# Attention's sums with the values taken over four query blocks instead of two, with the transposes one step later

## The chip, the core and the metric

The kernel runs on one core of a Trainium2 chip. The engines named here are PE (the matrix engine, TensorE), ACT (ScalarE), DVE (VectorE), POOL (GpSimd) and SP, which only issues DMAs. Each engine works through a queue of its own, in the order in which its instructions stand there. The metric is the device time of one execution in microseconds (us), taken as the median of several runs; lower is better.

## What is computed

One layer of a Griffin-style block on 1024 positions of width 1024, in float32: a stick-breaking attention with 16 heads of 64 channels and a gated short convolution side by side, each projected and gated, then an output projection and a SwiGLU FFN. The change concerns the attention:

```python
for i in range(s_len // Q_BLOCK):              # 8 query blocks of 128
    n_keys = (i + 1) * Q_BLOCK                 # causal: the keys up to and with this block
    z = einsum('bhqd,bhkd->bhqk', q[block i], k[:n_keys]) / sqrt(64)
    mask = s_idx < t_idx                       # strictly causal
    log_not = where(mask, log_sigmoid(-z), 0.0)
    excl = cumsum(log_not, reverse=True) - log_not
    a = where(mask, exp(log_sigmoid(z) + excl), 0.0)
    o[block i] = einsum('bhqk,bhkd->bhqd', a, v[:n_keys])
y = (sigmoid(ga) * (o @ w_branch_a) + sigmoid(gb) * (y_b @ w_branch_b))
```

## The kernel before

Every large product is made in split arithmetic: an operand is held as a high part (rounded to the engine's fp32r format) and a low part (the rest), and a product is the sum of two or three matmuls of 128 rows by up to 512 columns. A matmul with 512 columns is the largest that one PSUM bank takes.

The program is a sequence of stages: modulation and norm, the input projections, the attention (from 596 to 956 us of the span), the projection of branch a (`ya` times `w_a`), the output projection, the FFN. Its instructions are mixed with *fillers*: the convolution's gate and the product of branch b, matmuls of 512 columns into `pj`, in threes (lines 1026 to 1028).

A generator, `attention()`, goes through 128 steps, one for each head h and query block i, and issues in each:

- `att_scores(h, i)`: the scores `z` of block i against keys 0 to i, in pieces of at most 512 keys, two matmuls each (lines 921, 922). Steps i of 0 to 3 have one piece of 128 to 512 columns; steps 4 to 7 have one of 128 to 512 columns and one of 512. Each piece takes one of two PSUM banks (`NZ = 2`) and ACT turns it into sigmoids in `pt` (line 923), which frees the bank. POOL masks the diagonal.
- `att_scan(h, i)`: a running product on DVE (line 936) and one multiplication on POOL (line 133), after which `pt` holds the weights.
- `att_trans` of the step two steps back: PE transposes of those weights, 128x128 each, up to four into a bank `tr` (line 950, `NTR = 3` banks); ACT writes the high part `ath` (line 953) and DVE the low part `atl` (line 954).
- `att_av(h, g)`, three steps behind, in every second step: the sum with the values for the query blocks 2g and 2g+1 into a bank `o` of 256 columns, two matmuls for each key block (lines 965, 966), the stationary operand being the split values `vt` (high and low part side by side in 64 + 64 columns). The last key block concerns only the second query block, so its two matmuls have 128 columns. Then ACT takes out the upper 64 rows, adding `vlast` as bias (two instructions of 64x128, line 970, tile `otmp`), DVE adds the lower 64 rows (line 972, `oy`), and SP stores 64x256 to `d_ya`.

`att_dv` makes the `vt` of the next head in two parts, in steps 3 to 6 of the current one: ACT writes the high part (line 863), DVE the low part. `vt` has two buffers, so head h+1 gets the one that head h-1 used.

Between two yields of the generator the main loop issues fillers: a yield's number is a share of the fillers, and `fill` catches up to it. The order on PE is then pinned as issued, and that of the attention's own instructions on DVE and POOL too; ACT's and SP's order comes from the scheduler, which ranks by priority and expected readiness. Names in rows carry a running number (`z_9560`), which differs between the two builds.

## Time and profile before

| | |
|---|---|
| median of 3 runs (lowest, highest) | 1792.84 us (1792.69, 1794.17) |
| the profiled execution | 1792.41 us |
| its span in the trace | 1790.4 us |
| granted PE clock, mean | 1.00 |
| PE, DVE, ACT, POOL busy over the span | 1782.5, 1273.5, 830.9, 345.0 us |
| PE busy in 700 to 800 us (attention) | 99.87 us |
| DVE, ACT, POOL busy there | 80.09, 70.87, 39.04 us |

The time is what counts; the span is the part of it that the trace covers, and 2.0 us lie around it. Busy times are sums of instructions' durations. PE's instructions are pipelined: the next one starts before the one ahead has ended, so what a matmul costs is read from the distance of one start to the next, and a late operand can show as a long distance without any idle time beside it.

### The profile page before, as it was taken

Reading aid. Unit: us, or ns where it says so; the run is one execution under the profiler, and the core shown is the slowest. Engines: PE = TensorE matmul, PEld = TensorE weight load, DVE = VectorE, ACT = ScalarE, POOL = GpSimd, SP = SyncE. Lnnn points to the kernel's source line nnn. Section 1 sums busy time; section 2 is a strip of 40 time slices with the busy share of each in tenths; the row PEclk is TensorE's granted clock in tenths of the full one; section 3 lists DMA queues with packets and bytes.
Section 4 is the critical chain, followed back from the end, with each engine's and each line's share of the span. In section 5 each row is a group of like instructions: output and inputs, shape, how many; then the busy total and the mean of one; then the engine's idle time right before and its main releaser. Section 6 shows DMA issues by size and latency. Waiting matters only on the chain.

```text
span 1790.4 us, 24937 instructions
## 1 busy us (share of the span) xinstructions
PE 1782.5 (100%) x8611; PEld 1485.4 (83%) x8611; DVE 1273.5 (71%) x2030; ACT 830.9 (46%) x1555; POOL 345.0 (19%) x437
## 2 busy tenths in 40 slices
PE   9999999999999999999999999999999999999999
PEld 7888877888888888888888888888888888888887
DVE  6876586777874678777786864698867777644876
ACT  5534364333433567776675221764544444422321
POOL 0024334734231334333332100100000000000000
PEclk9999999999999999999999999999999999999999
DMA  9479654222634977796655856424534344389876
GB/s 383 162 248 381 240 185 165 77 94 100 225 130 147 298 197 191 218 324 172 166 136 176 308 194 212 129 95 169 208 130 148 147 183 157 137 316 345 276 236 220
DMA packets 165010, 359.09 MB, mean 201 GB/s; under 512 B 15538, under 2 KB 60938, under 8 KB 163732
## 3 DMA queue, kind: packets, MB, share of 16 engines
q1 hardware_dynamic: 128300, 289.65, 49.1%
q10 hardware_dynamic: 33096, 55.25, 8.7%
q0 software_dynamic: 3488, 12.59, 2.0%
q8 instruction: 69, 1.13, 0.3%
q14 instruction: 57, 0.47, 0.1%
HBM read 247.84 MB, written 109.62 MB: 200 GB/s over the span
## 4 chain that ended last, share of the span: by engine, by line
PE 96%; DMA 1%; DVE 1%; issue 0%; ACT 0%; POOL 0%; SPq 0%; POOLq 0%; DVEq 0%; ACTq 0%
PE e L129 8%; PE e L128 8%; PE e L127 8%; PE pj L127 7%; PE pj L128 7%; PE pj L129 7%; PE pj L294 7%; PE pj L1026 5%; PE pj L1028 5%; PE pj L1027 5%; PE e L1618 4%; PE e L1619 4%; PE e L1620 4%; PE tr L950 3%; PE o L966 2%; PE z L921 2%
## 5 line engine op out<-in xcount | busy, mean ns | idle before, releaser
L1234 ACT ACTIVATE whi<-raw 128x512 fp32r<-128x512 f32 x137 | 84.9, 628 | 160.6 <-PE e L128 99.8
L1235 DVE TENSOR_TENSOR wlo<-raw,whi 128x512 fp32r<-128x512 f32 x137 | 93.1, 687 | 70.6 <-ACT whi L1234 53.1
L133 POOL TENSOR_TENSOR pt<-pt 128x63 f32<-128x63 f32 (+7 forms) x128 | 101.6, 794 | 212.1 <-DVE pt L936 195.7
L128 PE MATMUL e<-big,whi 128*128 128x512 f32 x352 | 136.9, 389 | 0.0
L127 PE MATMUL e<-big,whi 128*128 128x512 f32 x352 | 136.5, 390 | 0.0
L129 PE MATMUL e<-big,wlo 128*128 128x512 f32 x352 | 136.1, 389 | 0.0
L294 PE MATMUL pj<-whi,big 128*128 128x512 f32 x448 | 132.6, 393 | 0.6 <-ACT big L263 0.4
L133 DVE TENSOR_TENSOR c<-pj,c 128x512 f32<-128x512 f32 x140 | 93.7, 684 | 53.9 <-PE pj L129 53.3
L954 DVE TENSOR_TENSOR atl<-tr,ath 128x512 fp32r<-128x512 f32 (+1 forms) x192 | 104.1, 553 | 35.6 <-ACT ath L953 34.2
L127 PE MATMUL pj<-big,whi 128*128 128x512 f32 x320 | 124.9, 390 | 0.0
L129 PE MATMUL pj<-big,wlo 128*128 128x512 f32 x320 | 124.7, 390 | 0.0
L128 PE MATMUL pj<-big,whi 128*128 128x512 f32 x320 | 124.6, 389 | 0.0
L1619 PE MATMUL e<-wlo,f 128*128 128x512 f32 (+1 forms) x319 | 121.9, 382 | 0.0
L1618 PE MATMUL e<-whi,f 128*128 128x512 f32 (+1 forms) x319 | 121.7, 382 | 0.0
L1620 PE MATMUL e<-whi,f 128*128 128x512 f32 (+1 forms) x319 | 121.6, 382 | 0.0
L923 ACT ACTIVATE pt<-z,rq 128x128 f32<-128x128 f32 (+1 forms) x192 | 107.2, 578 | 26.3 <-PE z L922 23.8
L524 ACT ACTIVATE whi<-raw 128x512 fp32r<-128x512 f32 x108 | 67.5, 629 | 109.0 <-PE pj L128 54.3
L133 DVE TENSOR_TENSOR wlo<-raw,whi 128x512 fp32r<-128x512 f32 x108 | 89.4, 831 | 36.2 <-ACT whi L524 36.1
L1026 PE MATMUL pj<-big,whi 128*128 128x512 f32 x256 | 113.3, 442 | 0.0
L953 ACT ACTIVATE ath<-tr 128x512 fp32r<-128x512 f32 (+1 forms) x192 | 93.2, 488 | 31.8 <-PE tr L950 30.8
L127 PE MATMUL e<-rh,whi 128*128 128x512 f32 x264 | 102.7, 389 | 0.0
L128 PE MATMUL e<-rl,whi 128*128 128x512 f32 x264 | 102.7, 389 | 0.0
(304 smaller groups left out, 4756.1 us busy)
## 6 DMA issues: line engine op xcount, KB each, us to landing
f<-d_f SPq DMA_DIRECT2D x77, 512.0 KB, 4.2
d_f<-fs SPq DMA_DIRECT2D x70, 512.0 KB, 2.6
raw<-w_cg SPq DMA_DIRECT2D x40, 512.0 KB, 4.1
raw<-w_u SPq DMA_DIRECT2D x26, 512.0 KB, 4.5
raw<-w_g SPq DMA_DIRECT2D x25, 512.0 KB, 3.4
raw<-w_kv SPq DMA_DIRECT2D x20, 512.0 KB, 5.2
ld<-ada SPq DMA_DIRECT2D x16, 512.0 KB, 8.7
d_t<-ts SPq DMA_DIRECT2D x16, 512.0 KB, 6.7
```

The costliest lines, as they stand in the source:

```text
L127: nc.tensor.matmul(ps, wh[:, k, :], fh[:, k, :], start=(k == 0 and not onto), stop=False, skip_group_check=onto)
L128: nc.tensor.matmul(ps, wh[:, k, :], fl[:, k, :], start=False, stop=False, skip_group_check=onto)
L129: last = nc.tensor.matmul(ps, wl[:, k, :], fh[:, k, :], start=False, stop=(k == 3), skip_group_check=onto)
L133: eng.tensor_tensor(out=out, in0=a, in1=b, op=op)
L294: nc.tensor.matmul(ps, a, b, start=(k == 0 and q == 0), stop=(k == KT - 1 and q == 2))
L923: nc.scalar.activation(pt[:, off + s0:off + s0 + m], z[:, :m], AF.Sigmoid, scale=rq[:, 1, i, h:h + 1])
L953: nc.scalar.activation(th[:, :nb, c0:c0 + P], src, AF.Copy)
L954: nc.vector.tensor_tensor(out=tl[:, :nb, c0:c0 + P], in0=src, in1=th[:, :nb, c0:c0 + P].bitcast(F32), op=ALU.subtract)
L1026: nc.tensor.matmul(ps, wh, rh_, start=(k == 0), stop=False)
L1618: nc.tensor.matmul(o, sh, w[0][:, c], start=(j == 0), stop=False)
L1619: nc.tensor.matmul(o, sh, w[1][:, c], start=False, stop=False)
L1620: nc.tensor.matmul(o, sl, w[0][:, c], start=False, stop=(j == NJ - 1))
```

## The change

The sum with the values now covers four query blocks at once (`o` of 512 columns; g is 0 or 1), in one group of key blocks that all four query blocks see (512 columns) and one that ends at the diagonal (512, 384, 256, 128 columns). The transposed weights get tiles of their own for the two groups: `afh`/`afl` (one buffer) for the first, `ath`/`atl` (two buffers) for the second. The transposes stand three steps behind the scores instead of two, and the sums four or more: `att_av` is now a generator that is advanced by pieces of two key blocks, so that the sum for g = 0 is made in step 7 of its head and step 1 of the next one, and that for g = 1 in steps 3 and 4 of the next head. The eviction is four ACT instructions of 64x128 into `oy` and one DVE addition of 64x512, with one store. `F_A` moves a share of 1.3 of the fillers from step 4 to step 1 in every head but the first. The reloads `yr` of branch a use four buffers of another pool that closes later, and the ring for software DMAs is given a size.

```diff
-    F_Z, F_T, F_S = 0.2, 0.3, 0.05
+    F_Z, F_T, F_S, F_A = 0.2, 0.3, 0.05, 1.3
...
-    def at_tile(tag):
-        return bp.tile([P, 4, 256], F32R, tag=tag, bufs=3, name=nm(tag))
+    def at_tile(full):
+        return tuple(bp.tile([P, (16 if full else 13) * P], F32R, tag=t_, bufs=1 if full else 2, name=nm(t_))
+                     for t_ in (("afh", "afl") if full else ("ath", "atl")))
...
-        yield F_Z + F_S * ((i - 1) % 8 + 1)
+        yield F_Z + F_S * ((i - 1) % 8 + 1) + (F_A if h and i == 1 else -F_A if h and i == 4 else 0)
...
     def att_trans(h, i):
         pt, off = ptof.pop((h, i)), D - (i + 1) * P
+        c = i % 4
         for b0 in range(0, i + 1, 4):
             nb = min(4, i + 1 - b0)
-            key = (h, i // 2, b0 // 4)
+            full = i // 4 > b0 // 4
+            key = (h, i // 4, full)
             if key not in ats:
-                ats[key] = (at_tile("ath"), at_tile("atl")) if ats else first_at
-            th, tl = ats[key]
+                ats[key] = first_at.pop(full) if full in first_at else at_tile(full)
             tr = pps.tile([P, 512], F32, tag="tr", bufs=NTR, name=nm("tr"))
             for j in range(nb):
                 nc.tensor.transpose(tr[:, j * P:(j + 1) * P], pt[:, off + (b0 + j) * P:off + (b0 + j + 1) * P], ident)
-            c0 = (i % 2) * P
+            u, f = (4, 0) if full else (3, c // 3)
+            th, tl = (t_[:, f * P:(4 * u + f) * P].rearrange("p (j t) -> p j t", t=u * P)[:, :nb, (c - f) * P:(c - f + 1) * P]
+                      for t_ in ats[key])
             src = tr[:, :nb * P].rearrange("p (j t) -> p j t", t=P)
-            nc.scalar.activation(th[:, :nb, c0:c0 + P], src, AF.Copy)
-            nc.vector.tensor_tensor(out=tl[:, :nb, c0:c0 + P], in0=src, in1=th[:, :nb, c0:c0 + P].bitcast(F32),
-                                    op=ALU.subtract)
+            nc.scalar.activation(th, src, AF.Copy)
+            nc.vector.tensor_tensor(out=tl, in0=src, in1=th.bitcast(F32), op=ALU.subtract)
             yield F_T * nb
...
     def att_av(h, g):
         pr, e0 = h // 2, (h % 2) * DH
         vt = vts[h]
-        o = pps.tile([P, 256], F32, tag="o", bufs=1, name=nm("o"))
-        for j in range(2 * g + 2):
-            c0 = P if j == 2 * g + 1 else 0
-            th, tl = ats[h, g, j // 4]
-            nc.tensor.matmul(o[:, c0:], vt[:, j, :], th[:, j % 4, c0:], start=(j == 0), stop=False)
-            lastav[0] = nc.tensor.matmul(o[:, c0:], vt[:, j, :], tl[:, j % 4, c0:], start=False, stop=(j == 2 * g + 1))
-        tmp = bp.tile([DH, 256], F32, tag="otmp", bufs=1, name=nm("otmp"))
-        yv = bp.tile([DH, 256], F32, tag="oy", bufs=3, name=nm("oy"))
-        for e in range(2):
-            nc.scalar.activation(tmp[:, e * P:(e + 1) * P], o[:DH, e * P:(e + 1) * P], AF.Identity,
-                                 bias=vlast[:, h, 2 * g + e:2 * g + e + 1])
-        nc.vector.tensor_tensor(out=yv, in0=o[DH:], in1=tmp, op=ALU.add)
-        hf, c0 = g // 2, (g % 2) * 256
-        nc.sync.dma_start(d_ya[hf][e0:e0 + DH, pr, c0:c0 + 256], yv)
+        o = pps.tile([P, 512], F32, tag="o", bufs=1, name=nm("o"))
+        for j in range(4 * g + 4):
+            full, d = j < 4 * g, j % 4
+            c0 = 0 if full else d * P
+            for e, t in enumerate(ats[h, g, full]):
+                lastav[0] = nc.tensor.matmul(o[:, c0:], vt[:, j, :], t[:, 4 * d * P:4 * d * P + 512 - c0],
+                                             start=(j + e == 0), stop=(j == 4 * g + 3 and e == 1))
+            if j % 2 and j < 4 * g + 3:
+                yield 0
+        yv = bp.tile([DH, 512], F32, tag="oy", bufs=2, name=nm("oy"))
+        for e in range(4):
+            nc.scalar.activation(yv[:, e * P:(e + 1) * P], o[:DH, e * P:(e + 1) * P], AF.Identity,
+                                 bias=vlast[:, h, 4 * g + e:4 * g + e + 1])
+        nc.vector.tensor_tensor(out=yv, in0=o[DH:], in1=yv, op=ALU.add)
+        nc.sync.dma_start(d_ya[g][e0:e0 + DH, pr, :], yv)
         yield 0
 
-    NZ, NTR, NPJ, DAV, KQ = 2, 3, 2, 3, 1
+    NZ, NTR, NPJ, DAV, KQ = 2, 3, 2, 4, 1
...
+        av = []
         steps = [(h, i) for h in range(H) for i in (LAST if h == H - 1 else ORDER)]
         for s in range(len(steps) + DAV):
...
                 yield from att_scores(h, i)
-            tr_ = att_trans(*steps[s - 2]) if 0 <= s - 2 < len(steps) else iter(())
-            av_ = att_av(steps[s - DAV][0], steps[s - DAV][1] // 2) if s >= DAV and s % 2 != DAV % 2 else iter(())
+            tr_ = att_trans(*steps[s - 3]) if 0 <= s - 3 < len(steps) else iter(())
+            if s >= DAV and steps[s - DAV][1] % 4 == 3:
+                av[:] = [att_av(steps[s - DAV][0], steps[s - DAV][1] // 4)]
             yield from itertools.islice(tr_, 1)
-            if s >= DAV and steps[s - DAV][1] == 5:
-                yield from av_
+            if s < len(steps):
+                yield from (a_ for q in av[:1] for a_ in itertools.islice(q, (0, 0, 0, 0, 1, 0, 0, 1)[s % 8]))
             yield from tr_
             if s < len(steps):
                 att_scan(*steps[s])
-            yield from av_
+            for q in av[:1]:
+                yield from itertools.islice(q, 9 if s >= len(steps) else (0, 2, 0, 2, 2, 0, 0, 2 * (s > 8 * H - 8))[s % 8])
...
+    def ya_slots():
+        for tag, bufs in (("va", 1), ("vb", 1), ("skl", 2), ("sq", 2), ("skh", 2), ("vt", 2), ("skl", 2), ("sq", 2), ("skh", 2)):
+            yield bp.tile([P, 2, 512], F32R, tag=tag, bufs=bufs, name=nm("ya"))
+        for t_ in at_tile(False):
+            yield t_[:, :1024].rearrange("p (e t) -> p e t", t=512)
+        for t_ in at_tile(True):
+            t_ = t_.rearrange("p (e t) -> p e t", t=512)
+            yield t_[:, :2]
+            yield t_[:, 2:]
+        yield bp.tile([P, 2, 512], F32R, tag="vt", bufs=2, name=nm("ya"))
...
+        for j, (ya2, (n, k)) in enumerate(zip(ya_slots(), [(0, k) for k in range(7)] + [(1, 0), (1, 1), (1, 2), (0, 7)] + [(1, k) for k in range(3, 8)])):
+            yr = fq.tile([P, 512], F32, tag=("ybh", "ybl")[j % 2], bufs=2, name=nm("yr"))
             nc.sync.dma_start(yr, d_ya[n][:, k, :])
-            ya2 = bp.tile([P, 2, 512], F32R, tag=tag, bufs=bufs, name=nm("ya"))
             h_, l_ = ya2[:, 0], ya2[:, 1]
...
+    fqpool.close()
+    sml = ExitStack()
+    mlp = sml.enter_context(tc.tile_pool(name="mlp", bufs=1, side="right", reuse_waits="tile"))
...
-    nc = bacc.Bacc("TRN2", target_bir_lowering=False, num_devices=1)
+    nc = bacc.Bacc("TRN2", target_bir_lowering=False, num_devices=1, dynamic_dma_scratch_size=2048)
```

What moves on PE, in step 4 and 5 around the end of a sum of head 12 in head 13. Ahead: the changed order, from the last matmul of the sum `o` on; `z_9096` and `z_9103` are the scores of step 5, `z_9121` and `z_9128` those of step 6, `pj` a filler.

```order
L969 MATMUL o_9053<-atl_8912,vt_8548 128x128
L922 MATMUL z_9096<-skh_8633,sqt_8632 128x256
L923 MATMUL z_9096<-skl_8634,sqt_8632 128x256
L922 MATMUL z_9103<-skh_8633,sqt_8632 128x512
L923 MATMUL z_9103<-skl_8634,sqt_8632 128x512
L952 MATMUL tr_9107<-dm,pt_5129 128x128 x3
L1033 MATMUL pj_9029<-big_7560,whi_8892 128x512
L1034 MATMUL pj_9029<-big_7561,whi_8892 128x512
L1035 MATMUL pj_9029<-big_7560,wlo_8893 128x512
L922 MATMUL z_9121<-skh_8633,sqt_8632 128x384
L923 MATMUL z_9121<-skl_8634,sqt_8632 128x384
L922 MATMUL z_9128<-skh_8633,sqt_8632 128x512
```

The order before at the same scores (`z_9560`, `z_9567` of step 5, `z_9586` of step 6), from the two last matmuls of a sum over two query blocks on:

```order
L965 MATMUL o_9549<-ath_9470,vt_9239 128x128
L966 MATMUL o_9549<-atl_9471,vt_9239 128x128
L921 MATMUL z_9560<-skh_9048,sqt_9047 128x256
L922 MATMUL z_9560<-skl_9049,sqt_9047 128x256
L921 MATMUL z_9567<-skh_9048,sqt_9047 128x512
L922 MATMUL z_9567<-skl_9049,sqt_9047 128x512
L950 MATMUL tr_9571<-dm,pt_5130 128x128 x4
L1026 MATMUL pj_9510<-big_7858,whi_9330 128x512
L1027 MATMUL pj_9510<-big_7859,whi_9330 128x512
L1028 MATMUL pj_9510<-big_7858,wlo_9331 128x512
L921 MATMUL z_9586<-skh_9048,sqt_9047 128x384
```

The second `z` of step 6, which stands right behind the first in the changed order, comes in the order before after another `pj` group. The transposes between are three instead of four.

ACT's queue at that place, first as changed, with the engines and DMA queues for which each instruction is to wait. The row with `vt` is the high part of the split values of head 14 (its buffer is that of head 12, `vt_8548`, which the sum above reads), those with `oy` are the evictions of that sum:

```order
L924 ACTIVATE pt_5131<-z_9070,rq 128x512 [waits PE_49,Activation_49]
L957 ACTIVATE ath_9045<-tr_9074 128x2x128 [waits PE_49]
L863 ACTIVATE vt_9118<-vb_8862 128x8x64 [waits DMAHW1_49,DVE_49,PE_49]
L975 ACTIVATE oy_9089<-o_9053,vlast 64x128 [waits DMAHW0_49]
L975 ACTIVATE oy_9089<-o_9053,vlast 64x128 x3
L924 ACTIVATE pt_5127<-z_9096,rq 128x256 [waits PE_49,Pool_49]
L924 ACTIVATE pt_5127<-z_9103,rq 128x512 [waits PE_49]
L957 ACTIVATE ath_9045<-tr_9107 128x3x128 [waits PE_49]
L924 ACTIVATE pt_5128<-z_9121,rq 128x384 [waits PE_49,Activation_49,Pool_49]
L924 ACTIVATE pt_5128<-z_9128,rq 128x512 [waits PE_49]
```

And before, where `otmp` is the eviction:

```order
L923 ACTIVATE pt_5131<-z_9529,rq 128x512 [waits PE_49]
L953 ACTIVATE ath_9536<-tr_9538 128x3x128 [waits DVE_49,PE_49]
L863 ACTIVATE vt_9583<-vb_9319 128x8x64 [waits DMAHW1_49,DVE_49]
L970 ACTIVATE otmp_9554<-o_9549,vlast 64x128 [waits PE_49,Activation_49]
L970 ACTIVATE otmp_9554<-o_9549,vlast 64x128
L923 ACTIVATE pt_5127<-z_9560,rq 128x256 [waits PE_49,Pool_49]
L923 ACTIVATE pt_5127<-z_9567,rq 128x512 [waits PE_49]
L953 ACTIVATE ath_9536<-tr_9571 128x4x128 [waits PE_49]
L524 ACTIVATE whi_10010<-raw_10008 128x512 [waits DMAHW3_49,PE_49]
L923 ACTIVATE pt_5128<-z_9586,rq 128x384 [waits PE_49,Pool_49]
```

The row of `vt` stands ahead of the evictions in both, but before it waits for DVE and a DMA, and after the change for PE as well, while the first eviction has no wait for PE of its own any more. The changed program has that wait for PE in 14 of its 16 `vt` rows, each of them right ahead of the evictions of g = 1; before, none of the 16 has it.

On PE in the first head, as changed, from the third step's filler on (`z_5304` belongs to step 3, `z_5317` and `z_5324` to step 4):

```order
L1033 MATMUL pj_5263<-big_144,whi_5150 128x512
L1034 MATMUL pj_5263<-big_146,whi_5150 128x512
L1035 MATMUL pj_5263<-big_144,wlo_5151 128x512
L922 MATMUL z_5304<-skh_5140,sqt_5139 128x512
L923 MATMUL z_5304<-skl_5141,sqt_5139 128x512
L952 MATMUL tr_5311<-dm,pt_5128 128x128
L922 MATMUL z_5317<-skh_5140,sqt_5139 128x128
L923 MATMUL z_5317<-skl_5141,sqt_5139 128x128
L922 MATMUL z_5324<-skh_5140,sqt_5139 128x512
L923 MATMUL z_5324<-skl_5141,sqt_5139 128x512
```

and before (`z_5306` belongs to step 3):

```order
L1026 MATMUL pj_5261<-big_144,whi_5148 128x512
L1027 MATMUL pj_5261<-big_146,whi_5148 128x512
L1028 MATMUL pj_5261<-big_144,wlo_5149 128x512
L950 MATMUL tr_5290<-dm,pt_5128 128x128
L921 MATMUL z_5306<-skh_5138,sqt_5137 128x512
L922 MATMUL z_5306<-skl_5139,sqt_5137 128x512
L950 MATMUL tr_5313<-dm,pt_5129 128x128 x2
L1026 MATMUL pj_5261<-big_144,whi_5148 128x512
L1027 MATMUL pj_5261<-big_146,whi_5148 128x512
L1028 MATMUL pj_5261<-big_144,wlo_5149 128x512
```

Before, the transposes of step 1's weights (`tr_5313`, of `pt_5129`) stand right behind the scores of step 3 and ahead of those of step 4; as changed, only one transpose (of step 0's weights) stands there and the next filler comes after the scores of step 4.

## Rows read from the trace of the kernel before

**Rows 1.** Page, part 1: engine, busy us (share of the span), instructions.

```profile
PE 1782.5 (100%) x8611; PEld 1485.4 (83%) x8611; DVE 1273.5 (71%) x2030; ACT 830.9 (46%) x1555; POOL 345.0 (19%) x437
```

**Rows 2.** Page, part 4: the chain that ended last, share by engine.

```profile
PE 96%; DMA 1%; DVE 1%; issue 0%; ACT 0%; POOL 0%; SPq 0%; POOLq 0%; DVEq 0%; ACTq 0%
```

**Rows 3.** PE's waits: engine line waited for, total us, times, longest.

```profile
PE tr L950 <- POOL pt L133: 0.9, 2, 0.5
```

**Rows 4.** Timeline, PE in attention: start us, duration us, engine, line, operation.

```profile
914.86 0.28 PE L966 MATMUL o<-atl,vt 128*128 128x256 f32 x1
914.98 0.22 PE L965 MATMUL o<-ath,vt 128*128 128x128 f32 x1
915.04 0.28 PE L966 MATMUL o<-atl,vt 128*128 128x128 f32 x1
915.15 0.51 PE L950 MATMUL tr<-dm,pt 128*128 128x128 f32 x3
...
921.01 0.45 PE L921 MATMUL z<-skh,sqt 128*128 128x512 f32 x1
921.29 0.39 PE L922 MATMUL z<-skl,sqt 128*128 128x512 f32 x1
```

**Rows 5.** Timeline, PE, third and fourth step of head 0.

```profile
599.11 0.40 PE L922 MATMUL z<-skl,sqt 128*128 128x512 f32 x1
600.01 0.44 PE L950 MATMUL tr<-dm,pt 128*128 128x128 f32 x2 [0.50 <-POOL pt L133]
```

**Rows 6.** Timeline, PE, a transpose later in attention.

```profile
682.21 0.40 PE L1028 MATMUL pj<-big,wlo 128*128 128x512 f32 x1
682.63 0.44 PE L950 MATMUL tr<-dm,pt 128*128 128x128 f32 x2
```

**Rows 7.** Timeline, PE, a sum with the values late in attention.

```profile
935.39 0.40 PE L1027 MATMUL pj<-big,whi 128*128 128x512 f32 x1
...
936.55 0.28 PE L965 MATMUL o<-ath,vt 128*128 128x256 f32 x1
937.15 0.38 PE L966 MATMUL o<-atl,vt 128*128 128x256 f32 x1 [0.32 <-DVE atl L954]
```

**Rows 8.** Timeline, all engines, an evicted sum and the scores behind it.

```profile
901.58 0.49 ACT L953 ACTIVATE ath<-tr 128x384 fp32r<-128x384 f32 x1 [0.34 <-PE tr L950]
...
901.97 0.62 ACT L863 ACTIVATE vt<-vb 128x512 fp32r<-128x512 f32 x1
...
902.11 0.56 DVE L954 TENSOR_TENSOR atl<-tr,ath 128x384 fp32r<-128x384 f32 x1 [0.21 <-ACT ath L953]
...
902.39 0.27 PE L966 MATMUL o<-atl,vt 128*128 128x128 f32 x1
...
902.76 0.61 ACT L970 ACTIVATE otmp<-o,vlast 64x128 f32<-64x128 f32 x2 [0.17 <-PE o L966]
...
903.25 0.60 PE L950 MATMUL tr<-dm,pt 128*128 128x128 f32 x4
903.27 1.03 ACT L923 ACTIVATE pt<-z,rq 128x256 f32<-128x256 f32 x2
...
903.61 0.48 PE L1026 MATMUL pj<-big,whi 128*128 128x512 f32 x1
...
904.39 0.34 PE L921 MATMUL z<-skh,sqt 128*128 128x384 f32 x1
```

**Rows 9.** Timeline, ACT, a split, two evictions and a sigmoid in a row.

```profile
944.65 0.63 ACT L1176 ACTIVATE ya<-yr 128x512 fp32r<-128x512 f32 x1 [1.15 <-PE o L966]
945.18 0.60 ACT L970 ACTIVATE otmp<-o,vlast 64x128 f32<-64x128 f32 x2
945.68 0.68 ACT L923 ACTIVATE pt<-z,rq 128x512 f32<-128x512 f32 x1
```

**Rows 10.** Timeline, PE's last sum with the values and DVE's last `ya`.

```profile
977.53 0.27 PE L966 MATMUL o<-atl,vt 128*128 128x128 f32 x1
...
988.36 0.69 DVE L133 TENSOR_TENSOR ya<-yr,ya 128x512 fp32r<-128x512 f32 x1 [0.46 <-ACT ya L1176]
```

More of the change, by code (lines that the diff above doesn't have):

```diff
@@ L896, in block_kernel @@
     first_vl = bp.tile([9, 512], F32, tag="vl", bufs=1, name=nm("vl"))
-    first_at = (at_tile("ath"), at_tile("atl"))
+    first_at = {True: at_tile(True), False: at_tile(False)}
     first_va = v_tile(1)
@@ L1130, in block_kernel @@
             prev[i.engine] = i
-    fqpool.close()
-    sml = ExitStack()
-    mlp = sml.enter_context(tc.tile_pool(name="mlp", bufs=1, side="right", reuse_waits="tile"))
     def mods_last():
@@ L1164, in preload_wo @@
                 w_pre.append((hi, lo))
-    slots = [("va", 1), ("vb", 1), ("skl", 2), ("sq", 2), ("skh", 2), ("vt", 2), ("skl", 2), ("sq", 2), ("skh", 2),
-             ("ath", 3), ("atl", 3), ("ath", 3), ("atl", 3), ("ath", 3), ("atl", 3), ("vt", 2)]
+    def ya_slots():
[8 more added lines that the diff above has]
+        yield bp.tile([P, 2, 512], F32R, tag="vt", bufs=2, name=nm("ya"))
     yah, yal = ([[None] * KT for n in range(2)] for e in range(2))
     with tc.high_priority():
-        for (tag, bufs), (n, k) in zip(slots, [(0, k) for k in range(7)] + [(1, 0), (1, 1), (1, 2), (0, 7)] + [(1, k) for k in range(3, 8)]):
-            yr = fp.tile([P, 512], F32, tag="yr", bufs=3, name=nm("yr"))
+        for j, (ya2, (n, k)) in enumerate(zip(ya_slots(), [(0, k) for k in range(7)] + [(1, 0), (1, 1), (1, 2), (0, 7)] + [(1, k) for k in range(3, 8)])):
+            yr = fq.tile([P, 512], F32, tag=("ybh", "ybl")[j % 2], bufs=2, name=nm("yr"))
             nc.sync.dma_start(yr, d_ya[n][:, k, :])
-            ya2 = bp.tile([P, 2, 512], F32R, tag=tag, bufs=bufs, name=nm("ya"))
             h_, l_ = ya2[:, 0], ya2[:, 1]
```

## The prediction

> **What bounds the kernel now.** I read the page's first part before anything else: PE is busy for 1782.5 of 1790.4 us [rows 1]. The chain that ended last says the same from the other side, 96% of it are PE's own instructions [rows 2]. So a microsecond counts only if it is taken from PE's row of starts or put into it. The list of PE's waits is nearly empty; of the attention it holds two waits of the transposes for POOL, 0.9 us together, the longest 0.5 [rows 3]. Hence the third view, the timeline of the attention, read by the distance from one start to the next: there a matmul of 512 columns takes 0.23 us (five in 1.16, from 935.39 to 936.55) [rows 7], one of 256 columns 0.12, and a pair of 128 columns 0.06 and 0.11 [rows 4]. Last I looked at ACT, which has slack on average (70.87 of 100 us between 700 and 800) but works in order, and which alone sets free the two banks into which the scores go.
>
> **The sums with the values.** The multiplied columns are the same; the number of matmuls falls. Before, the 16 heads make 512 matmuls of 256 columns and 64 pairs of 128 (a pair for each sum). In rows: 512 x 0.12 = 61.4; a pair of 128 is followed by a matmul whose successor comes 0.28 behind it instead of 0.23 [rows 4], so a pair costs 0.06 + 0.11 + 0.05 = 0.22 and the 64 pairs 14.1; together 75.5 us. After, there are 192 matmuls of 512 columns at 0.232 (44.5), 64 of 384 at 0.176, halfway between the two sizes (11.3), 64 of 256 at 0.12 (7.7) and 32 pairs of 128 (7.0): 70.5. **Minus 5.0.** Bounds: if the 0.05 behind a pair belongs to the matmul that follows and stays, minus 3.4; minus 5.4 if the 512 columns take 0.23.
>
> **Transposes one step later.** In head 0 the second transpose group waits for POOL: 0.90 from start to start instead of 0.23 [rows 5], 0.67 lost, of which the trace marks 0.50. Two such waits with 0.9 marked [rows 3] make about 1.24 with 0.17 unmarked in each. With a step more they go. What is late next there is a bank: `z_5324` needs the bank of `z_5304`, with one transpose and two 128-column matmuls in between and no filler. After the low matmul of `z_5304` starts, its sigmoid may start 0.37 later (as the eviction does after the last sum, 902.39 to 902.76) [rows 8] and takes 0.68 [rows 9]; 0.04 for the hand-over, as from `ath`'s end at 902.07 to `atl` at 902.11 [rows 8]; so 1.09, against 0.23 + 0.11 + 0.06 + 0.11 = 0.51 of work. A new wait of 0.6: **minus 0.6** net. Further on, a transpose now and then comes late without a mark, 0.42 instead of 0.23 [rows 6]; I count three such, 0.6 together. One sum waits 0.5 for its low part on DVE (0.60 from start to start instead of 0.12) [rows 7]. With operands a step older both kinds should go: **minus 1.1** (0 if others take their place).
>
> **A new wait on ACT.** This is the term that decides. In the changed order the split of head h+1's values (`vt`) is to wait for PE: its buffer is that of head h-1, whose sum now ends in step 4 of head h. It stands ahead of the four evictions of that very sum, and these ahead of the sigmoids of step 5. Before, the split ran at 901.97 while PE was still at the sum, and the eviction began 0.37 after the sum's last start [rows 8]. After, from that last start as zero:
> - the split starts at 0.37 and the next ACT instruction 0.53 later (944.65 to 945.18) [rows 9], so the evictions start at 0.90;
> - four evictions at 0.255 each (902.76 to 903.27 for two) [rows 8]: the two sigmoids of step 5 start at 1.92;
> - the pair takes 1.03 [rows 8] and ends at 2.95; with 0.04 for the hand-over the second bank is free at 2.99.
>
> PE's plan: before, the scores of step 6 start 2.00 after the sum's last matmul (902.39 to 904.39), with two pieces of scores, four transposes (0.36, 903.25 to 903.61) and a filler group in between [rows 8]. After there are three transposes, so 1.91; and the second piece of step 6 now stands right behind the first (two matmuls of 384 columns, 0.35), at 2.26. It takes the second bank: 2.99 - 2.26 = **0.73 late, per head**. About 0.5 of it falls on the first piece, which needs the bank of the 256-column sigmoid, the rest on the second. Fourteen heads have such a split: **plus 10.2**. Nothing behind gives it back, since PE has no gaps from which to. Bounds: 0.6 per head if PE releases ACT 0.1 earlier than 0.37 and evictions overlap a little more (plus 8.4); 0.85 if evictions take 0.27 and PE needs a moment to restart (plus 11.9). The Trainium skill has a price for the eviction, on the page ScalarE: Activation LUTs, section "What ACT_TABLE_LOAD costs": an ACTIVATE with a pointer bias takes about 280 ns plus 0.833 ns per element, and back-to-back ones overlap by about 93 ns. As an estimate from that page an eviction of 128 columns would be spaced 0.294, four of them 0.16 later in all, and the term plus 12.4; the row has 0.255, and the sum goes by the row.
>
> **What I cost at nothing.** The transposes' count and the scores are unchanged. Filler moved from step 4 to step 1 is the same work; its price is the missing cover in step 6, counted above. DVE's one addition per sum in place of two, and half the stores, lie beside PE. The last sum's way to branch a: before, the last `ya` was ready 11.5 us after the last sum began to end (977.53 to 989.05) [rows 10]; after, 61 matmuls of 512 columns, 14 us, stand between the last sum and the first product that reads that tile, so two more evictions (0.5) still fit; if the load came 4 us later, 1.5 us would show. The other pool for `yr` and the DMA ring touch transfers which that same work covers.
>
> **Sum**, against the profiled execution: 1792.41 - 5.0 - 0.6 - 1.1 + 10.2 = 1795.9. That execution lies 0.4 below the median of the runs; against the median, **1796.3 us**, 0.2% slower. A measurement of this kernel tells a change from none from about 0.2%, 3.6 us, so this stands just at the edge.
>
> **Rivals.**
> - *The split is no obstacle* (its wait is over early, as before, or it slips behind the evictions): then the sigmoids of step 5 start 0.53 earlier, the pair ends at 2.42 and the second bank is free at 2.46, 0.2 late per head, plus 2.8: about 1789. For it: before, ACT is never held by the split, and the wait in the order doesn't say how long it is. Against it: the first eviction has no wait for PE of its own left, so the split's must reach to the sum's last matmul. 0.14.
> - *ACT's lateness does not reach PE at all*, and only the gain stays: 1792.8 - 6.7 = 1786, **faster**. Its place is the same pair of banks; it happens if the second piece of step 6 finds its bank free, that is if release, split, evictions and sigmoids take 2.2 us instead of 2.95. The point from which the change gains more than 0.2% is a lateness under (6.7 - 3.6) / 14 = 0.22 per head, against my 0.73. For it: ACT's busy share of 71%, and that the profile before shows no wait of PE for a bank of scores. Against it: each of the durations is read from a row. 0.14, and in the same direction 0.01 for the next.
> - *A matmul costs less in long ones than its columns say.* The Trainium skill, page TensorE: Matmul & The Clock Gate, section "Back-to-back issue gap", has 131 ns for a sustained 512-column matmul against 81 for 128 columns. By estimate from that the sums would fall from about 60 us to about 43, a gain three times mine. What the rows show is 0.232 and 0.06 to 0.11, in proportion to columns, and this decides. If 512 columns should be cheaper only in the new pieces, say 0.13, the sum would fall by 20 us to 1776: 0.01.
> - *More than I see*: further waits of the same kind in step 1, where the first sum of a head is evicted, or of the transposes for DVE, whose queue now holds an addition that waits for four evictions. With 0.3 per head more: 1800.5. 0.07.
>
> **How the numbers follow.** The likeliest case, split ahead of evictions and PE late for the banks, has 0.64; its own range, from the bounds of its terms (8.4 to 11.9, minus 6.7 to 3.4 or less), is 1794 to 1799.5. It lies across the edge of 0.2%: I give 0.36 to slower and 0.28 to no difference. The first rival lies at the other edge, half and half: 0.07 the same, 0.07 faster. The second and third add 0.15 to faster, the fourth 0.07 to slower. Slower 0.43, same 0.35, faster 0.22. The range from 1788 to 1800 leaves out the second and third rivals (0.15) and part of the fourth.
>
> **What the profile after will show.** Right: a split of `vt` on ACT that starts about 0.35 after the sum's last matmul, with idle time before it that PE ended; distances of 0.7 and 0.4 instead of 0.23 and 0.18 ahead of the two pieces of step 6; waits of PE's `z` for ACT in the list, 14 times. The sums with 512 columns at 0.23. Head 0's waits for POOL gone, a bank wait in their place. Wrong: a split that runs before the sum ends; scores of step 6 that start within 2.3 of the sum's end; the gain in sums under 3 us; PE waiting at the first products with `ya`.

## The result and the profile after

The changed kernel takes 1800.27 us (median of 6 runs, 1797.59 to 1801.60) against 1793.47 us for the kernel before on the same chip: a ratio of 1.0036, 95% interval 1.0025 to 1.0047. It is slower, by 6.8 us; the forecast was 1796.3, in a range from 1788 to 1800. The median lies 0.3 above that range as it stands; by the ratio, against the 1792.84 us that the forecast goes by, it is 1799.3, just inside. The profiled execution took 1801.09 us with a span of 1799.3, 8.9 us more than the one before.

The page's first part and the chain that ended last, which answer to [rows 1, 2]:

```profile
PE 1784.4 (99%) x8355; PEld 1469.4 (82%) x8355; DVE 1266.2 (70%) x1998; ACT 826.8 (46%) x1555; POOL 343.1 (19%) x437
...
PE 92%; DMA 3%; DVE 2%; ACT 2%; issue 0%; SPq 0%; POOL 0%; DVEq 0%; POOLq 0%; ACTq 0%
```

PE's share of the chain falls from 96 to 92%: other engines now stand between PE's instructions. PE's waits (columns: engine and line, released by, us in total, times, longest), which answer to [rows 3]:

```profile
PE z L922 <- ACT pt L924: 5.1, 16, 0.5
...
PE o L969 <- DVE atl L958: 0.6, 1, 0.6
PE tr L952 <- DVE afl L958: 0.5, 1, 0.5
PE pj L1033 <- ACT ya L1186: 0.5, 1, 0.5
...
PE pj L1034 <- DVE ya L133: 0.2, 1, 0.2
```

The first row is new: 16 waits of the scores for ACT's sigmoids, which free their banks (fourteen of one pattern, a like one in the last head, and one in head 0). One of them in its surroundings, around the end of head 12's sum, on all engines (start, duration, engine, line); it answers to [rows 8]:

```profile
906.93 0.27 PE L969 MATMUL o<-atl,vt 128*128 128x128 f32 x1
...
907.25 0.63 ACT L863 ACTIVATE vt<-vb 128x512 fp32r<-128x512 f32 x1 [0.43 <-PE o L969]
...
907.78 1.11 ACT L975 ACTIVATE oy<-o,vlast 64x128 f32<-64x128 f32 x4
...
908.61 0.40 PE L1035 MATMUL pj<-big,wlo 128*128 128x512 f32 x1
908.78 1.04 ACT L924 ACTIVATE pt<-z,rq 128x256 f32<-128x256 f32 x2
...
909.30 0.19 PEld L922 LDWEIGHTS z<-skh,sqt 128*128 128x128 f32 x1 [0.74 <-ACT pt L924]
...
909.58 0.33 PE L923 MATMUL z<-skl,sqt 128*128 128x384 f32 x1
...
909.88 0.19 PEld L922 LDWEIGHTS z<-skh,sqt 128*128 128x128 f32 x1 [0.28 <-ACT pt L924]
...
910.21 0.40 PE L923 MATMUL z<-skl,sqt 128*128 128x512 f32 x1
```

To be read from the sum's last matmul at 906.93: the split `vt` starts 0.32 later, the four evictions at 0.85, the two sigmoids of step 5 at 1.85, and they end at 2.89. The first piece of step 6 starts 0.69 after the matmul ahead of it, where 0.23 is the rule: 0.46 late. The second starts at 2.95, and each of the two is followed by its partner 0.10 later than the columns cost (0.28 instead of 0.18, 0.33 instead of 0.23). When the partner starts, PE is 0.79 behind. This pattern comes in fourteen heads. It comes once more, with 0.58, in the last head, which has no `vt` to split; there ACT splits a reloaded `ya` between the evictions and the sigmoids:

```profile
955.14 0.63 ACT L1186 ACTIVATE ya<-yr 128x512 fp32r<-128x512 f32 x1
```

Together these are 11.6 us. In the view of line 863 (the split), the idle time of ACT before it and who ended it:

```profile
  PE o L969: 5.5, 13
```

Over the stretch from the first score of the attention to the last product with `ya` the kernel lost 8.3 us (596.06 to 1063.08 before, 595.93 to 1071.22 after). The recurring lateness took 11.6; single waits took 4.9, against 2.5 before; what is left over for the sums over four blocks is a gain of 5.7. Added up directly, from start to start and without their late operands, the matmuls of the sums take 71.1 us against 75.3, a gain of 4.2; what stands behind a pair of 128 columns is 0.05 late as before, but 32 times less often, which makes 1.6 more.

### The profile page after: what moved, and what is told of

Read it like the earlier page. It is cut to its first block, busy times and chain, and to the rows that moved or that the text cites. A ratio compares the mean times of both kernels' runs of the same rounds, so it can differ in the third digit from the quotient of the medians.

```text
span 1799.3 us, 24284 instructions
## 1 busy us (share of the span) xinstructions
PE 1784.4 (99%) x8355; PEld 1469.4 (82%) x8355; DVE 1266.2 (70%) x1998; ACT 826.8 (46%) x1555; POOL 343.1 (19%) x437
## 4 chain that ended last, share of the span: by engine, by line
PE 92%; DMA 3%; DVE 2%; ACT 2%; issue 0%; SPq 0%; POOL 0%; DVEq 0%; POOLq 0%; ACTq 0%
PE pj L294 8%; PE e L127 8%; PE e L128 8%; PE e L129 8%; PE pj L127 7%; PE pj L129 7%; PE pj L128 7%; PE pj L1033 4%; PE pj L1034 4%; PE pj L1035 4%; PE o L969 4%; PE e L1633 3%; PE e L1631 3%; PE e L1632 3%; PE tr L952 3%; PE z L922 2%
## 5 line engine op out<-in xcount | busy, mean ns | idle before, releaser
L937 DVE TENSOR_TENSOR_SCAN pt<-pt 128x64 f32<-128x64 f32 (+7 forms) x128 | 95.9, 749 | 11.7 <-POOL pt L927 11.4
L129 PE MATMUL e<-rh,wlo 128*128 128x512 f32 x264 | 102.0, 389 | 0.0
```

Of the source, the lines that this page charges most:

```text
L129: last = nc.tensor.matmul(ps, wl[:, k, :], fh[:, k, :], start=False, stop=(k == 3), skip_group_check=onto)
L937: nc.vector.tensor_tensor_scan(out=both, data0=first, data1=both, initial=1.0, op0=ALU.mult, op1=ALU.mult)
```

## The experiments

All times are medians of three to five rounds; ratios are to the kernel before on the same chip (1793.3 to 1793.9 us in these sets, close enough to compare kernels of different sets by their times).

**The split out of the way, in two ways.** First by its place in the program:

```diff
-                    if s % 8 in ((4, 6) if h % 2 else (3, 5)) and h + 1 < H:
-                        att_dv(h + 1, s % 8 // 5)
+                    if s % 8 in (5, 6) and h + 1 < H:
+                        att_dv(h + 1, s % 8 - 5)
```

> The changed kernel with the two parts of the values' split issued in steps 5 and 6 for every head (before: 3 and 5, or 4 and 6), so that the split stands behind the evictions on ACT and has no wait for PE of its own. Split theory (the split's wait for the end of the sum holds up evictions and sigmoids): the lateness of the step-6 scores falls from about 0.8 us per head to about 0.25, so the kernel gets 8 us faster than the changed one, about 1792. Rival, lost cover (the scores of step 6 are late since filler was taken from step 4): lateness and time unchanged, about 1800. Rival, four evictions instead of two: lateness falls by no more than 0.3 per head, 1796.

Measured: 1796.44 us, ratio 1.0017 (1.0008 to 1.0026), half of the gain that was expected. Of the recurring lateness of 0.79, 0.27 is left in thirteen of the fourteen heads, but PE's list shows the same engines with fewer and longer waits:

```profile
PE z L922 <- ACT pt L924: 3.2, 4, 1.3
PE tr L952 <- DVE afl L958: 2.8, 3, 1.4
```

and ACT's list of the attention (596 to 960 us) one that was 0.8 us before and 3.2 after the change:

```profile
ACT whi L524 <- DMA raw<-w_cg: 6.5, 3, 3.5
```

ACT stands at the split of a filler's weights that are still on their way from memory, and what is queued behind it (transposed weights, sigmoids) is late for PE. So the mechanism of the split is borne out, and about half of what its removal should bring is lost to single waits (8.1 us of longer distances in this trace against 4.9 in the changed kernel's).

The second way leaves the place and gives the split another buffer:

```diff
-        vt = vts[h] = bp.tile([P, KT, P], F32R, tag="vt", bufs=2, name=nm("vt"))
+        vt = vts[h] = bp.tile([P, KT, P], F32R, tag="vt", bufs=3, name=nm("vt"))
...
-        yv = bp.tile([DH, 512], F32, tag="oy", bufs=2, name=nm("oy"))
+        yv = bp.tile([DH, 512], F32, tag="oy", bufs=1, name=nm("oy"))
```

> The changed kernel with three buffers for the split values (and one instead of two for the evicted sums, to make room). The split keeps its place in the program but needs no sum to end. Split theory: the split runs while PE is still at the sum, or wherever the scheduler puts it, with no idle time on ACT before it that PE ends; lateness of the step-6 scores 0.25 per head or less; about 1791. Rival, lost cover: no change, 1800. If the single buffer of the evicted sums costs something, ACT waits for a DMA ahead of an eviction.

Measured: 1795.59 us, ratio 1.0012 (1.0003 to 1.0021). That is 4 us short of the expectation. There is no idle time of ACT ahead of the split that PE ends, and the recurring lateness is down to 0.3 per head; but ACT waits 2.9 us for stores ahead of evictions, 3.1 for weights, and single waits of PE of up to 1.3 us appear. The third kernel of this kind keeps two buffers for the sums; the room comes from the ring for software DMAs:

```diff
-        yv = bp.tile([DH, 512], F32, tag="oy", bufs=1, name=nm("oy"))
+        yv = bp.tile([DH, 512], F32, tag="oy", bufs=2, name=nm("oy"))
...
-    nc = bacc.Bacc("TRN2", target_bir_lowering=False, num_devices=1, dynamic_dma_scratch_size=2048)
+    nc = bacc.Bacc("TRN2", target_bir_lowering=False, num_devices=1, dynamic_dma_scratch_size=512)
```

> The changed kernel with three buffers for the split values while the evicted sums keep two; the room comes from the ring for software DMAs, 512 instead of 2048 bytes. In the run with one buffer for the sums, ACT waited 2.9 us for stores ahead of evictions and the time was 1795.6. Split theory: step-6 scores late by at most 0.25 per head and ACT's waits for stores gone, 1793. If irregular waits of ACT for the fillers' weights and of PE for DVE carry the rest, they stay, some 4 to 6 us, and the time stays at 1795.

Measured: 1792.10 us, ratio 0.9991 (0.9982 to 0.9999): 8 us faster than the changed kernel. (A smaller ring by itself was not run.) The same place in its timeline:

```profile
900.32 0.27 PE L969 MATMUL o<-atl,vt 128*128 128x128 f32 x1
...
900.63 1.12 ACT L975 ACTIVATE oy<-o,vlast 64x128 f32<-64x128 f32 x4
...
901.64 1.04 ACT L924 ACTIVATE pt<-z,rq 128x256 f32<-128x256 f32 x2
...
902.22 0.38 PE L922 MATMUL z<-skh,sqt 128*128 128x384 f32 x1
902.44 0.34 PE L923 MATMUL z<-skl,sqt 128*128 128x384 f32 x1
...
902.74 0.19 PEld L922 LDWEIGHTS z<-skh,sqt 128*128 128x128 f32 x1 [0.28 <-ACT pt L924]
...
903.08 0.39 PE L923 MATMUL z<-skl,sqt 128*128 128x512 f32 x1
```

The evictions start 0.31 after the sum's last matmul, the first piece of step 6 is on time at 1.90, its second matmul comes 0.05 late, and the second piece waits 0.12 and is followed 0.10 late: 0.27 per head, where the first rival of the prediction has 0.2.

**Cover.** The filler shift undone:

```diff
-    F_Z, F_T, F_S, F_A = 0.2, 0.3, 0.05, 1.3
+    F_Z, F_T, F_S, F_A = 0.2, 0.3, 0.05, 0.0
```

> The changed kernel with the filler shift F_A set to 0, so that the groups moved to step 1 are back in step 4. Rival, lost cover: the lateness of the step-6 scores goes, about 1790. Split theory: the filler comes back ahead of the sum's last matmuls and not behind them, so the distance from the sum's end to the step-6 scores is as it was, the lateness stays at 0.8 per head and the time within 3 us of the changed kernel's 1800; what may change is step 1, which loses cover (up to 0.3 per head slower).

Measured: 1797.06 us, ratio 1.0020 (1.0011 to 1.0028), 3 us faster than the changed kernel. This one speaks for both theories. In eleven heads one filler group stands between the sum's end and the step-6 scores, as in the changed kernel, and the wait is there in all eleven. In the first four, `fill` catches up a group later and two groups stand there; PE and ACT in one of these:

```profile
648.97 0.28 PE L969 MATMUL o<-atl,vt 128*128 128x128 f32 x1
...
649.28 0.63 ACT L863 ACTIVATE vt<-vb 128x512 fp32r<-128x512 f32 x1 [0.85 <-PE o L969]
...
649.82 1.10 ACT L975 ACTIVATE oy<-o,vlast 64x128 f32<-64x128 f32 x4
...
650.82 1.04 ACT L924 ACTIVATE pt<-z,rq 128x256 f32<-128x256 f32 x2
...
651.56 0.34 PE L922 MATMUL z<-skh,sqt 128*128 128x384 f32 x1
...
651.73 0.34 PE L923 MATMUL z<-skl,sqt 128*128 128x384 f32 x1
651.91 0.50 PE L922 MATMUL z<-skh,sqt 128*128 128x512 f32 x1
652.25 0.39 PE L923 MATMUL z<-skl,sqt 128*128 128x512 f32 x1
```

The split, evictions and sigmoids come at 0.31, 0.85 and 1.85 after the sum's last matmul, just as late as in the changed kernel, and yet the first piece of step 6 starts on time at 651.56 and the second 0.35 behind it at 651.91, because PE had 0.7 us more to do; only the last matmul, 0.34 behind, is still 0.11 late. The lateness is ACT's chain minus PE's cover; less of the one or more of the other takes it away.

One filler group moved between the two pieces of step 6 (a share of 1.1 given there and taken from behind the step):

```diff
             if s0:
-                yield F_Z
+                yield F_Z + (1.1 if i == 6 else 0)
-        yield F_Z + F_S * ((i - 1) % 8 + 1) + (F_A if h and i == 1 else -F_A if h and i == 4 else 0)
+        yield F_Z + F_S * ((i - 1) % 8 + 1) + (F_A if h and i == 1 else -F_A if h and i == 4 else -1.1 if i == 6 else 0)
```

> The changed kernel with one group of three filler matmuls moved from behind the second piece of the step-6 scores to between the two pieces. The split theory as worked out for the two banks: the first piece still waits 0.5 for the 256-column sigmoid; the second has 0.7 more time and its wait of 0.1 and the 0.1 after it go. About 0.2 per head, 3 us faster than the changed kernel: 1797. If the second piece's lateness is the whole of it: 1789.

Measured: 1797.10 us, ratio 1.0019 (1.0010 to 1.0029), the 3 us that the two banks, taken apart, are worth. The first piece in its timeline still starts 0.70 after the filler and is followed 0.10 late; then nothing is late any more:

```profile
906.12 0.40 PE L1035 MATMUL pj<-big,wlo 128*128 128x512 f32 x1
906.82 0.44 PE L922 MATMUL z<-skh,sqt 128*128 128x384 f32 x1 [0.30 <-ACT pt L924]
907.10 0.33 PE L923 MATMUL z<-skl,sqt 128*128 128x384 f32 x1
907.26 0.40 PE L1033 MATMUL pj<-big,whi 128*128 128x512 f32 x1
```

**The evictions alone.** One instruction in place of four:

```diff
-        for e in range(4):
-            nc.scalar.activation(yv[:, e * P:(e + 1) * P], o[:DH, e * P:(e + 1) * P], AF.Identity,
-                                 bias=vlast[:, h, 4 * g + e:4 * g + e + 1])
+        nc.scalar.activation(yv, o[:DH], AF.Identity, bias=vlast[:, h, 4 * g:4 * g + 1])
```

> The changed kernel with a single ACT eviction of 64x512 per sum instead of four of 64x128; it takes the bias of the first query block for all four, so that part of the output is another. The split's wait stays. Split theory with the chain as summed (split, evictions, two sigmoids, one after the other): the evictions shrink from 1.02 to about 0.55, so the step-6 scores are late by 0.3 per head instead of 0.8 and the kernel is 7 us faster than the changed one, about 1793. If the evictions do not stand in that chain: no change, 1800.

Measured: 1792.99 us, ratio 0.9993 (0.9983 to 1.0002), 7 us faster. The split's wait stays (ACT idle 5.3 us ahead of it), the eviction takes 0.57 to the next instruction, and PE's recurring lateness falls to 0.35. So the split's 0.53 and the evictions' 1.0 stand in one chain and each part is worth its length.

**The transposes' step alone**, on the kernel before, and undone in the changed one:

```diff
# the kernel before
-    NZ, NTR, NPJ, DAV, KQ = 2, 3, 2, 3, 1
+    NZ, NTR, NPJ, DAV, KQ = 2, 3, 2, 4, 1
...
-            tr_ = att_trans(*steps[s - 2]) if 0 <= s - 2 < len(steps) else iter(())
+            tr_ = att_trans(*steps[s - 3]) if 0 <= s - 3 < len(steps) else iter(())
# the changed kernel: the second pair of lines the other way round
```

> The kernel before with one part of the change alone: transposes three steps behind the scores and the sums over two query blocks four steps behind. My terms: the two waits of head 0 for POOL go and a wait for a bank comes (minus 0.6), the small late operands go (minus 1.1), the work is the same: 1.7 us faster than before, 1791.6. A split that here too has to wait for a sum (every second head has one in the order) would show as ACT idle before it, but two evictions and a filler group between the scores leave PE covered. Rival: a step more makes DVE's or ACT's queue collide somewhere else, same or slower than before.

Measured: 1794.98 us, ratio 1.0003 (0.9995 to 1.0012): no gain, as the rival had it. The two waits for POOL are gone and the bank's wait of 0.7 is there, as worked out, and the late operands of before are gone; but a sum waits 1.05 and another 0.51 for a low part from DVE in the first head, a third 0.49 later, and four scores are 0.23 late each.

> The changed kernel with the transposes two steps behind the scores, as before the change, and the sums as changed. My terms: the step more was worth 1.7 us (two waits for POOL in head 0, late operands), so this is 1.7 slower than the changed kernel, about 1802. In the run of the kernel before with the step more there was no such gain, 1.4 slower if anything; by that this one is the same as the changed kernel or faster, 1798 to 1800. The 14 waits for a bank of scores stay in either case.

Measured: 1798.96 us, ratio 1.0029 (1.0018 to 1.0039), the same as the changed kernel within what both spread. Its waits of PE:

```profile
PE tr L952 <- POOL pt L133: 2.1, 7, 0.5
...
PE o L969 <- ACT afh L957: 1.7, 1, 1.7
PE z L922 <- ACT pt L924: 1.4, 7, 0.2
```

The median is that of the changed kernel, but what makes it up is not, and neither expectation saw it. The step-6 scores are late in six heads only, by 0.46 each and twice by 0.2 more (3.2 us instead of 11.6), since in the nine others two filler groups stand behind the sum, and everywhere four transposes instead of three. That is the layout before the change: there too the same nine heads have two groups (2.70 us from the sum's last matmul to the scores), and only the six others have one, as in [rows 8]. Before, in one of the nine:

```profile
649.28 0.28 PE L966 MATMUL o<-atl,vt 128*128 128x128 f32 x1
...
651.99 0.34 PE L921 MATMUL z<-skh,sqt 128*128 128x384 f32 x1
```

The changed kernel has one in all fifteen. So in nine heads the wait costs something only because cover was taken away as well, and it is the transposes' step that took it: this kernel differs from the changed one in nothing else. What the two groups save here is lost to the transposes: seven marked waits for POOL, 0.2 to 0.3 without a mark ahead of a sum in thirteen heads, and 1.8 at one place near the last sum. So with sums over two blocks the step more is worth nothing, and with sums over four it is worth, by estimate, some 5 us (the two differences of bank waits and medians, 8.4 and 1.3 us, leave 7.1, less the 1.8 near the last sum).

**The single waits.** The kernel with three buffers and two sums, with filler between the pieces, and without the hold on the convolution gate's weights:

```diff
-                with tc.issue_after(lastld[0].ins) if m > 1 else ExitStack():
+                with ExitStack():
                     cb_w[m] = load_ch(w_cg[0, m])
```

> As the kernel with three buffers and two sums, and besides with one filler group between the two pieces of the step-6 scores and with the loads of the convolution gate's weights no longer held behind the loads of the heads' values. Theory of the irregular rest (ACT stands at a filler's weights that are still on their way, and PE waits for what is behind them): ACT's wait for those weights falls from 3 to 7 us to under 1, PE's irregular waits to about 3 us, and the kernel comes to about 1789, faster than before. Rival: the weights' loads are late for another reason, or the waits only move; 1793 to 1796.

Measured: 1797.20 us, ratio 1.0020 (1.0011 to 1.0029): 5 us slower than the kernel with three buffers and two sums, against the expectation, and 7 slower than the same kernel with the hold, which follows below. ACT's wait for the weights is gone, and between 621 and 930 us PE waits nowhere for longer than 0.15. But the weights now go ahead of the first head's keys. PE at the start of the attention:

```profile
595.72 0.39 PE L1035 MATMUL pj<-big,wlo 128*128 128x512 f32 x1
599.73 0.30 PE L922 MATMUL z<-skh,sqt 128*128 128x128 f32 x1 [3.62 <-DMA skh<-d_k]
...
602.59 0.63 PE L1034 MATMUL pj<-big,whi 128*128 128x512 f32 x1
603.02 0.63 PE L1035 MATMUL pj<-big,wlo 128*128 128x512 f32 x1
```

and the same stretch in the view by windows (engines' busy us with counts, the granted PE clock, DMA share, GB/s):

```profile
600.00:607.00 7.00, 6.03 (x25) 4.92 (x24) 2.73 (x6) 2.24 (x6) 1.13 (x3) 0.54 1.13 250
```

PE stands for 3.8 us, and what follows takes 0.43 per 512 columns instead of 0.23: the granted clock is 0.54 from 600 to 607 us, mostly the lower of the two levels (1.2 GHz), after PE had been idle. Together some 8 us, more than the freed waits were worth.

With the hold, and with the filler between the pieces:

> The kernel with three buffers for the split values (two for the evicted sums, smaller DMA ring), and one filler group between the two pieces of the step-6 scores. In the run without the latter, each of 14 heads still showed 0.12 of waiting and 0.10 after it at the second piece. Split theory: these 0.22 per head go, 3 us faster than that run's 1792.1, so 1789, clear of the kernel before. Rival: irregular waits take their place, 1792.

Measured: 1790.32 us, ratio 0.9982 (0.9973 to 0.9991). **Faster than both kernels**: 3.3 us below the one before, 10 below the changed one. Of the recurring lateness 0.05 per head is left, and of the single waits 4.5 us together.

Two changes more, against two single waits seen in the earlier kernels:

```diff
-        nc.sync.dma_start(d_ya[g][e0:e0 + DH, pr, :], yv)
+        (nc.scalar if (h, g) == (H - 1, 1) else nc.sync).dma_start(d_ya[g][e0:e0 + DH, pr, :], yv)
# and a share of 1.1 of the fillers from step 5 to step 3 of head 0
```

> As the kernel with three buffers and filler between the pieces, and with two of the remaining single waits taken away: the last store of a sum is issued from ACT's queue instead of SP's, where it stood behind reloads that wait for other work (1.2 us of PE's waiting at the first product with the last tile), and one filler group of head 0 moves from step 5 to step 3, between the scores that share a bank (0.7 to 1.1 us). If each is worth what the trace shows: 2 us faster than without them, 1787. If the waits move on: the same as without them.

Measured: 1790.52 us, ratio 0.9982 (0.9973 to 0.9991): no difference. The wait for the last `ya` was no test: in the trace of the kernel that this one is built on, PE is late there by 0.15 only. The first head's bank wait is gone, and a sum in that head now waits 1.06 for DVE instead of 0.40, a score in the next one 1.11 instead of 0.43. The waits move on.

And the hold kept only for the blocks 2 and 3 of the weights (`m in (2, 3)` for `m > 1`):

> The kernel with three buffers and filler between the pieces (1790.3 us), and with the later loads of the convolution gate's weights (output blocks 4 to 7) no longer held behind the loads of the heads' values; those of blocks 2 and 3, which in the earlier run went ahead of the first head's keys, stay held. Theory: ACT's wait for weights falls from 4.7 us to under 2, PE's single waits between 629 and 680 us (1.4 us together) go, the first head is not held up: 1 to 1.5 us faster, 1789. Rival: the loads go ahead of other heads' keys or the waits move on: 1790 or more.

Measured: 1790.34 us, ratio 0.9981 (0.9972 to 0.9990), not told apart from the 1790.32. ACT's wait for weights is gone and with it PE's two waits at 662 and 674 us; its profile has the wait for the last `ya` instead (1.05).

## Why the prediction was right, and where its sizes were off

**The mechanism that decided was right, in place and size.** The split's wait for the end of the sum, four evictions, two sigmoids, and PE at the bank: predicted at 0.37, 0.90, 1.92 and 2.99 after the sum's last matmul, measured at 0.32, 0.85, 1.85 and 2.95. The lateness was 0.79 per head instead of 0.73: the chain ended 0.04 earlier, and after the second wait PE needed 0.10 more to the next start, which the prediction had only in its upper bound. PE's cover was read from one of the six heads with 2.00 us [rows 8]; that suits the changed order, which has one filler group everywhere, but the nine heads with 2.70 lost a group, and the prediction put that down to the filler that `F_A` moves. A fifteenth head, where the split of `ya` stands in the chain, was not counted. The term plus 10.2 measured 11.6. Without the split's wait the lateness is 0.27 (the first rival had 0.2); with two filler groups it is 0.1.

**The sums** were put at minus 5.0; they measured minus 5.7 as what is left over in the stretch, and 4.2 and 1.6 counted directly. So columns at 0.232 per 512 hold for the new pieces too; at the end of head 12's sum 256 columns take 0.12 (906.76 to 906.88) and the last pair 0.05 and 0.11, close to [rows 4]. The rule of the Trainium skill that would have put the gain three times as high (TensorE: Matmul & The Clock Gate, "Back-to-back issue gap") does not hold here. The eviction's price stayed with the row too: four take 1.00, 0.25 each, not the 0.294 that the prediction estimated from the Trainium skill (ScalarE: Activation LUTs, "What ACT_TABLE_LOAD costs").

**The step that failed** is "with operands a step older both kinds should go: minus 1.1". The minus 0.6 beside it held: in head 0 the waits for POOL went, and the bank's wait came as worked out (0.72 of lost time), minus 0.5 net:

```profile
599.26 0.27 PE L923 MATMUL z<-skl,sqt 128*128 128x128 f32 x1
600.04 0.50 PE L922 MATMUL z<-skh,sqt 128*128 128x512 f32 x1 [0.50 <-ACT pt L924]
```

The four late operands of before (1.2 us) did go too, but five others came, of 0.81, 0.67, 0.57, 0.50 and 0.27, on sums and transposes that wait for DVE: plus 1.6 instead of minus 1.1. This is nearer to the fourth rival's waits for DVE, but they came singly, three of them in heads 0 and 1, and not in every head. With the bank's wait and 1.2 us behind the last sum (below) they make up nearly all of the 4.9 us of single waits; before, the waits for POOL and the four late operands were the 2.5. One of them, on ACT, DVE and PE:

```profile
660.95 0.63 ACT L524 ACTIVATE whi<-raw 128x512 fp32r<-128x512 f32 x1 [3.15 <-DMA raw<-w_cg]
...
661.62 0.69 DVE L133 TENSOR_TENSOR wlo<-raw,whi 128x512 fp32r<-128x512 f32 x1 [3.10 <-PE z L923]
...
662.22 0.28 DVE L958 TENSOR_TENSOR atl<-tr,ath 128x128 fp32r<-128x128 f32 x1
...
662.65 0.52 PE L952 MATMUL tr<-dm,pt 128*128 128x128 f32 x3 [0.34 <-DVE atl L958]
```

ACT's split of a filler's weights waits 3.15 us for its DMA; DVE's low part of these weights stands ahead of `atl`, and the transposes wait 0.50 for the bank that `atl` frees. The kernel before with the step alone shows that the distance by itself gains nothing (its waits at 611 and 617 us come with it); with the sums over four blocks the transposes wait for POOL again without it. The kernels with the weights' loads show that ACT's queue, held at a DMA, sets some of these waits. The others (a sum or a transpose for DVE in heads 0 and 1, and at 930 us among the reloads of `ya`) moved from one kernel to the next and were not traced to one cause.

**What was costed at nothing** held but for the way from the last sum to branch a. The last sum's last matmul starts at 984.62:

```profile
984.62 0.27 PE L969 MATMUL o<-atl,vt 128*128 128x128 f32 x1
...
991.33 0.45 SPq L978 DMA_DIRECT2D d_ya<-oy  x1
...
995.73 0.32 SPq L1184 DMA_DIRECT2D yr<-d_ya  x1
...
999.29 0.50 PE L1033 MATMUL pj<-ya,whi 128*128 128x512 f32 x1 [0.48 <-ACT ya L1186]
```

The store is issued 6.7 us after the sum, behind reloads on SP's queue that wait for other work, and the reload of the tile another 4.4 later; PE reaches its product and waits 1.2 in all, near the 1.5 given for a load 4 us late. The prediction had named such a wait as a sign of being wrong. It is not in every kernel with the same order: the run with the split late has no such wait.

**The size of the whole** was forecast at plus 3.5 and measured at plus 6.8, near twice that. The terms, forecast and measured: 10.2 and 11.6 for ACT's chain, minus 5.0 and minus 5.8 for the sums, minus 0.6 and minus 0.5 for head 0, minus 1.1 and plus 1.6 for late operands, 0 and 1.2 behind the last sum. That the result still lies at the end of the range owes something to its width. The narrower range of the likeliest case, 1794 to 1799.5, left out that case's own bound of 0 for the operands; with it, and with the sums at minus 3.4, the case reaches 1800.7.

**What is left over.** The terms by rows add up to 8.1, close to the 8.3 by which the stretch is longer and to the span's 8.9. The medians differ by 6.8; the changed kernel's runs spread over 4 us and the profiled one is near their upper end, so its single waits are likely above the usual. That was not shown run by run.

## To carry to other kernels

When work is put off, ask which buffer it still holds and what is queued behind the instruction that wants that buffer. Here a small copy inherited a wait for PE, and because ACT works in order, the copy held up the sigmoids that free PE's banks; the average load of ACT (71%) said nothing about it, the order with its waits did. A chain like that is compared with the work that PE has until it needs the result: one buffer more, or 0.7 us of filler in the right gap, each took away most of the lateness here, and the saving in matmuls showed only then.

## What was not expected of the hardware

After a wait for a bank, the next start of PE came 0.10 us late, every time (0.28 instead of 0.18 at 384 columns, 0.33 instead of 0.23 at 512), also where the wait itself was only 0.12. And an idle stretch of 3.8 us at the start of the attention was followed by a granted clock of 0.54 over the next 7 us, with 0.43 us per 512 columns in it instead of 0.23.
